# One level of Strassen's algorithm in the w1 and w3 products of a dense feed-forward stack

## The chip, the cores and the metric

One core of one Trainium2 chip runs the whole program. The metric is the device time of one execution in microseconds, as the median over several runs.

## The reference, cut to what matters

The program is a recurrent block with a mixture of experts, and behind it a second block of two layers. Each of these layers has a feed-forward part, a mixer (short convolution, Fourier branch, pooling, gates) and a second feed-forward part. The change concerns the four feed-forward parts.

```python
def swiglu(h, w1, w3, w2):
    return (jax.nn.silu(h @ w1) * (h @ w3)) @ w2

for l in range(DEPTH_2):                       # 2 layers
    h = rmsnorm(x, g_ffn1[l])
    x = x + 0.5 * swiglu(h, w1_a[l], w3_a[l], w2_a[l])
    h = rmsnorm(x, g_mix[l])
    ...
    x = x + merged @ w_o[l]
    h = rmsnorm(x, g_ffn2[l])
    x = x + 0.5 * swiglu(h, w1_b[l], w3_b[l], w2_b[l])
return rmsnorm(x, g_final)
```

There are 512 tokens, the model width is 1024 and the feed-forward width is 2816. Everything is float32.

## The kernel before, in words

**Precision.** A product of float32 is made of three matmuls on reduced-precision operands: each operand is held as a high part and a low part (what the high part leaves), and `mm3` (L170) adds high by high, high by low and low by high. ScalarE casts the high part, VectorE subtracts to get the low part.

**Layout.** Features are on the partitions and the 512 tokens are the columns. The residual x is eight tiles `X[0..7]` of 128 features by 512 tokens. Width 2816 makes 22 feature tiles.

**Weights.** They come as blocks of 128 x 2048 (1 MB) in the order of use; `Stream` (L67) holds the list. `_dma` (L99) issues a block on SP's queue when a raw buffer is free (two of them in the dense phase); `_split` (L119) turns half a block (128 x 1024) into `whi` (ScalarE, L135) and `wlo` (VectorE, L136), in five pairs of buffers; `advance` (L154) is called behind the matmuls on a half and splits as far ahead as the buffers allow, four halves.

**The order of the work** is the order in which the code emits it: each engine runs its own queue in order, and waits where an operand is not ready.

**A feed-forward part** (`ffn`, L1309). The gain is folded into the operand: `prep` (L1213) casts x times gain into `xgh` and `xgl` for each tile as soon as that tile of x is final, and `square` (L1206) sums the squares, ScalarE squaring and POOL adding. `in_chunk` (L1253) multiplies one feature tile of w1 or of w3, eight tiles of x by `mm3`, into one bank. The reciprocal root of the mean square comes late: `rstd_1` (L1226) and `rstd_2` (L1239) run behind the second and third chunk and give `R`, a token a column. For each feature tile VectorE multiplies both products by R (L1334, L1336), ScalarE takes the Silu (L1335), VectorE multiplies (L1337), and `hilo` (L1185) splits the hidden tile. After 12 feature tiles `out_part` (L1261) multiplies them with w2, output tile by output tile, and VectorE adds half of the product to `X[j]` (L1342); then the same with the other 10 tiles. Behind the last addition to a tile the next part's `prep` follows.

**The mixer** (L1347) ends in `out_part2` (L1285), which multiplies four tiles at a time with w_o, the last of the four three output tiles later; VectorE adds to `X[j]` (L1486), and the second feed-forward part's `prep` follows.

**PSUM.** Eight banks, used in turn by `bank` (L1176). SBUF tiles of 128 x 512 come from `tmp` (seven) and `slot` (thirty).

Of the kernel before, what the change touches and what calls it, by code (L numbers as in the profile page):

```python
# [21 lines left out]
S = 512  # L22
# [10 lines left out]
NFA = 12  # L33
L2 = 2
LAG2 = 3
# [31 lines left out]
class Stream:  # L67
    """Weight blocks of 128 x 2048 in the order of use: DMA, then each half as hi + lo."""

    def __init__(self, tc, wpool, nr, nh):  # L70
        self.tc, self.nc = tc, tc.nc
        self.pool = wpool
        self.nh = nh
        self.slots = []
        self.gate = self.hold = 1 << 30
        self.slots_from(wpool, "raw", nr)
        self.blocks = []
        self.raw = {}
        self.half = {}
        self.nb = 0  # L80
        self.ns = 0

    def slots_from(self, pool, tag, n, lo=0, hi=1 << 30, bufs=None):
        """n more raw buffers, for blocks lo to hi"""
        new = [dict(pool=pool, tag=tag, bufs=bufs or n, blk=None, lo=lo, hi=hi) for _ in range(n)]
# [3 lines left out]
    def add(self, aps, keep=()):  # L89
        """keep: blocks that are not split but read as they come"""  # L90
        self.blocks += aps
        self.keep = set(keep)
        self.used = set()

    def _free(self, s):
        b = s["blk"]
        return b is None or (b in self.used if b in self.keep else 2 * b + 1 < self.ns)

    def _dma(self):  # L99
        while self.nb < min(len(self.blocks), self.gate):  # L100
            free = [s for s in self.slots if s["lo"] <= self.nb < s["hi"] and self._free(s)]
# [5 lines left out]
            t = s["pool"].tile([128, BLK], F32, name=s["tag"], tag=s["tag"], bufs=s["bufs"])  # L107
            if self.nb == 0:
                self.first = [lambda a=a, b=b: self.nc.sync.dma_start(t[:, a:b], self.blocks[0][:, a:b])
                              for a, b in FIRST]  # L110
            else:
                self.nc.sync.dma_start(t, self.blocks[self.nb])
# [5 lines left out]

    def _split(self, late=None):  # L119
        h = self.ns  # L120
        if h >= 2 * len(self.blocks):
            return False
        self._dma()
        assert h // 2 < self.nb
        src = self.raw[h // 2][:, (h % 2) * HB:(h % 2 + 1) * HB]
        self.ns += 1
        if h // 2 in self.keep:
# [9 lines left out]
        f() if late is None else late.append(f)  # L137
        return True

    def split_first(self, i):  # L140
        """A piece of the first half"""
# [12 lines left out]
    def advance(self, h, defer=False):  # L154
        """Everything of half h (and before) has been emitted. defer: returns the low parts still to be emitted"""
        late = []
        self.used |= {b for b in self.keep if 2 * b + 1 <= h}
        while self.ns < min(2 * len(self.blocks), self.hold):
            ahead = sum(q // 2 not in self.keep for q in range(h + 1, self.ns + 1))
            if ahead > self.nh - 1 or self.ns // 2 >= self.nb + 1:  # L160
                break
            self._dma()
            if self.ns // 2 >= self.nb:
# [6 lines left out]
def mm3(nc, ps, w, x, first, last):  # L170
    (wh, wl), (xh, xl) = w, x
    nc.tensor.matmul(ps, wh, xh, start=first, stop=False)  # L172
    nc.tensor.matmul(ps, wh, xl, start=False, stop=False)  # L173
    nc.tensor.matmul(ps, wl, xh, start=False, stop=last)  # L174


def build(tc, A):
    nc = tc.nc
    ctx = ExitStack()
    with ctx:  # L180
# [22 lines left out]
        order += [YD[c * 256:(c + 1) * 256].rearrange("(p k) d -> p (k d)", k=2) for c in range(4)]  # L203
        for l in range(L2):
            for n, b in ((N_FFN + 8, None), (N_MIX - 2, A["dfts"])):
                if b is not None:
                    order.append(b)
                order += [wb[i] for i in range(pos, pos + n)]
                pos += n
            order += [wb[i] for i in range(pos, pos + N_FFN)]  # L210
            pos += N_FFN
# [28 lines left out]
        K = dict(tc=tc, A=A, C=C, XP=XP, st=st, vec=vec, vc=vc, vr=vr, ident=ident, onesf=onesf, YD=YD, cs=cs)  # L240
# [47 lines left out]
def rec_phase(K):  # L288
# [256 lines left out]
    # the first of two token tiles is ahead of the second at the end  # L545
# [1175 lines left out]
```

## Time and profile before

| What | us |
|---|---|
| runs, median | 3047.95 |
| runs, lowest and highest | 3045.75, 3051.06 |
| profiled execution, first to last instruction (its span) | 3045.3 |
| TensorE matmuls busy in it | 2972.5 (98%) |
| VectorE busy | 1743.2 (57%) |
| ScalarE busy | 1302.1 (43%) |
| POOL busy | 282.3 (9%) |

The times of the table's last five lines are of one profiled execution, and so are all rows below. Its span is the time from its first to its last instruction; its own device time, as a run would give it, is not listed beside it. Busy shares are means over stages with different limits. A matmul's listed duration includes the time in which its last columns leave the array, so that listed durations of neighbours overlap: how fast matmuls follow each other is read from their starts.

### The profile page before, as it was taken

What the parts mean: (1) busy time and instruction counts of PE and PEld (TensorE: products, weight loads), DVE (VectorE), ACT (ScalarE), POOL (GpSimd) and SP (SyncE); (2) the same over time, 40 slices, a digit from 0 to 9 for tenths busy, and PEclk for the clock granted to TensorE, in tenths of its full rate; (3) what the DMA queues carried; (4) which work ended last, traced back from release to release, by engine and by line L of the source; (5) the groups of instructions that cost most, each with busy time, mean ns of one, the idle gap of its engine ahead of it and who ended that gap; (6) DMA issues with size and microseconds to landing.
All of it is one profiled execution on the core that took longest, in us unless ns stands there. A gap on an engine that the chain in (4) does not pass through costs nothing.

```text
span 3045.3 us, 33566 instructions
## 1 busy us (share of the span) xinstructions
PE 2972.5 (98%) x13360; PEld 2338.3 (77%) x13360; DVE 1743.2 (57%) x2127; ACT 1302.1 (43%) x1687; POOL 282.3 (9%) x235
## 2 busy tenths in 40 slices
PE   9997999999899999999999999999999999999998
PEld 7875666666568888888878888888888888878887
DVE  7678888898974344455555334443344465544343
ACT  4746888888753223233233223322223332332222
POOL 0025222220600000000010000100001000100002
PEclk9998999999999999999999999999999999999999
DMA  6374899999822222222222222222222222232221
GB/s 191 119 277 171 342 363 347 373 371 374 319 80 88 96 97 97 92 81 105 97 97 97 97 97 83 97 97 96 99 83 97 83 97 100 94 109 86 96 97 56
DMA packets 75360, 452.18 MB, mean 148 GB/s; under 512 B 8684, under 2 KB 19308, under 8 KB 22336
## 3 DMA queue, kind: packets, MB, share of 16 engines
q1 hardware_dynamic: 71040, 441.78, 39.4%
q0 software_dynamic: 3072, 7.17, 0.6%
q8 instruction: 106, 1.74, 0.2%
q10 hardware_dynamic: 1088, 1.05, 0.1%
q14 instruction: 54, 0.44, 0.0%
HBM read 439.79 MB, written 14.16 MB: 149 GB/s over the span
## 4 chain that ended last, share of the span: by engine, by line
PE 77%; DVE 4%; ACT 2%; issue 1%; POOL 0%; POOLq 0%; DVEq 0%; ACTq 0%
PE mm L172 23%; PE mm L173 23%; PE mm L174 23%; DVE wlo L136 2%; PE y L857 2%; PE h L822 2%; PE h L821 1%; ACT whi L135 1%; PE ht L835 1%; PE gat L792 1%; DVE xgl L1224 0%; DVE z L1064 0%; DVE X L1486 0%; PE h L824 0%; ACT X L1114 0%
## 5 line engine op out<-in xcount | busy, mean ns | idle before, releaser
L136 DVE TENSOR_TENSOR wlo<-raw,whi 128x1024 fp32r<-128x1024 f32 x533 | 663.9, 1255 | 432.3 <-ACT whi L135 432.3
L172 PE MATMUL mm<-xgh,whi 128*128 128x512 f32 x2048 | 810.6, 396 | 2.2 <-ACT xgh L1218 2.2
L173 PE MATMUL mm<-xgl,whi 128*128 128x512 f32 x2048 | 809.8, 395 | 2.1 <-DVE xgl L1224 2.1
L174 PE MATMUL mm<-xgh,wlo 128*128 128x512 f32 x2048 | 809.2, 395 | 0.0
L135 ACT ACTIVATE whi<-raw 128x1024 fp32r<-128x1024 f32 x535 | 557.9, 1052 | 498.3 <-PE mm L173 457.3
L173 PEld LDWEIGHTS mm<-xgl,whi 128*128 128x128 f32 x2048 | 386.1, 189 | 94.5 <-DVE xgl L1224 4.3
L172 PEld LDWEIGHTS mm<-xgh,whi 128*128 128x128 f32 x2048 | 386.2, 189 | 93.1 <-ACT xgh L1218 2.6
L174 PEld LDWEIGHTS mm<-xgh,wlo 128*128 128x128 f32 x2048 | 386.1, 189 | 90.7
L172 PE MATMUL mm<-s,whi 128*128 128x512 f32 (+1 forms) x938 | 368.0, 392 | 0.0
L173 PE MATMUL mm<-s,whi 128*128 128x512 f32 (+1 forms) x938 | 367.9, 392 | 0.0
L174 PE MATMUL mm<-s,wlo 128*128 128x512 f32 (+1 forms) x938 | 367.8, 392 | 0.0
L1187 ACT ACTIVATE s<-t 128x512 fp32r<-128x512 f32 x128 | 81.0, 633 | 376.2 <-DVE t L1337 298.8
L1211 POOL TENSOR_TENSOR ssum<-ssum,t 128x512 f32<-128x512 f32 x41 | 57.0, 1391 | 1740.2 <-ACT t L1208 1739.5
L136 DVE TENSOR_TENSOR wlo<-rawb,whi 128x1024 fp32r<-128x1024 f32 x162 | 203.6, 1298 | 22.7 <-ACT whi L135 20.6
L172 PEld LDWEIGHTS mm<-s,whi 128*128 128x128 f32 x938 | 176.6, 188 | 40.8
L173 PEld LDWEIGHTS mm<-s,whi 128*128 128x128 f32 x938 | 176.6, 188 | 40.8
L174 PEld LDWEIGHTS mm<-s,wlo 128*128 128x128 f32 x938 | 176.6, 188 | 40.6
L822 PE MATMUL h<-wlo,xt 128*64 128x512 f32 x512 | 195.6, 402 | 7.0 <-DVE wlo L136 6.3
L1336 DVE TENSOR_TENSOR t<-mm,R 128x512 f32<-128x512 f32 x88 | 60.8, 691 | 224.4 <-PE mm L174 224.4
L821 PE MATMUL h<-whi,xt 128*128 128x512 f32 x448 | 181.4, 405 | 5.9 <-PEq L1033 5.0
L1342 DVE SCALAR_TENSOR_TENSOR X<-mm,X 128x512 f32<-128x512 f32 x63 | 43.6, 692 | 227.8 <-PE mm L174 227.8
L857 PE MATMUL y<-whi,hd 128*64 128x512 f32 x512 | 161.6, 397 | 2.5 <-ACT whi L135 1.5
(356 smaller groups left out, 3281.7 us busy)
## 6 DMA issues: line engine op xcount, KB each, us to landing
raw<-in_wblocks SPq DMA_DIRECT2D x265, 1024.0 KB, 4.8
rawb<-in_wblocks SPq DMA_DIRECT2D x81, 1024.0 KB, 6.8
rawa<-in_wblocks SPq DMA_DIRECT2D x57, 1024.0 KB, 6.6
YD<-cs SPq DMA_DIRECT2D x8, 512.0 KB, 7.3
xt<-in_wblocks SPq DMA_DIRECT2D x4, 1024.0 KB, 8.3
rawb<-YD SPq DMA_DIRECT2D x3, 1024.0 KB, 4.8
z<-in_x POOLq DMA_DIRECT2D x4, 512.0 KB, 9.3
raw<-in_dfts SPq DMA_DIRECT2D x2, 1024.0 KB, 4.8
```

What stands on the lines that cost most here:

```text
L135: self.nc.scalar.activation(hi, src, AF.Copy)
L136: f = lambda E=self.nc.vector: E.tensor_tensor(lo, src, hi, op=OP.subtract)
L172: nc.tensor.matmul(ps, wh, xh, start=first, stop=False)
L173: nc.tensor.matmul(ps, wh, xl, start=False, stop=False)
L174: nc.tensor.matmul(ps, wl, xh, start=False, stop=last)
L821: nc.tensor.matmul(ps, x, w[0][:, sl], start=k == 0, stop=False)
L822: nc.tensor.matmul(ps[:64], x[:, 0:64], w[1][:, sl], start=False, stop=False)
L857: nc.tensor.matmul(ps[i][:64], hd[:, f, v:v + 64], w[wv][:, sl], start=f == 0 and n == 0, stop=f == 3 and n == 2)
L1187: act(hi, src, AF.Copy)
L1211: late.append(lambda: E.tensor_tensor(ssum, ssum, t, op=OP.add))
L1336: TT(v, p3, R, op=OP.mult)
L1342: STT(X[j], ps, 0.5, X[j], op0=OP.mult, op1=OP.add)
```

## The change

For a pair of feature tiles of w1 (and of w3) the weights are cut into four quarters of 128 output features by 512 input features, and the input into four quarters of 512 features by 256 tokens. Seven products of sums of quarters replace eight products of quarters (Winograd's form). One such pair is a `group`: seven steps, each with one half block of weights and 4 x 2 x 3 = 24 matmuls of 256 columns, for w1 in the left half of a bank and for w3 in the right.

- **Weights.** `Stream` now has entries that differ from the halves as they lie in memory. For the two blocks p and q of a group it loads q whole and adds half of p to it (an accumulating transfer on POOL's queue); p whole; and half of q with half of p added, into a buffer of half size. Two further sums are made by VectorE in the raw buffer. Seven halves per group are split into high and low, where it was four. There is one more raw buffer of full size and one of half size in a feed-forward part.
- **Inputs.** `forms` makes the sums of quarters of x and their high and low parts, for two tiles of x (k and k + 4) at a time, behind the second one's last addition; `gained` applies the gain, `prep_s` takes the place of `prep` ahead of these parts. The tiles of x are now finished in the order 0, 4, 1, 5, 2, 6, 3, 7.
- **Products.** Three of the seven are accumulated on copies of others, which ScalarE makes from bank to bank; VectorE makes the remaining differences, times R. The end of a group is emitted among the next one's steps.
- **Chunks.** The 22 feature tiles go in chunks of 6, 8 and 8 instead of 12 and 10, and the first two output tiles of a chunk leave their last two hidden tiles for later. The first six tiles of the first feed-forward part keep the old form.
- **Memory.** Six banks in turn and two for the copies; `slot` has 45 tiles, `tmp` five in a feed-forward part and seven in the mixer.

The diff, cut to its core:

```diff
-NFA = 12
+CH = ((0, 6), (6, 14), (14, 22))
+JO = (0, 4, 1, 5, 2, 6, 3, 7)
...
+            p, q = it
+            a = self._block(BLK, (0, BLK, q, False), (0, HB, p[:, HB:], True))
+            b = self._block(BLK, (0, BLK, p, False))
+            c = self._block(HB, (0, HB, q[:, :HB], False), (0, HB, p[:, :HB], True))
+            self._ent(a, 0)
+            self._ent(b, 0)
+            self._ent(a, 0, (b, 0))
+            self._ent(b, 1)
+            self._ent(a, 0, (a, 1))
+            self._ent(c, 0)
+            self._ent(a, 1)
...
-                self.nc.sync.dma_start(t, self.blocks[self.nb])
+                for x, y, src, more in loads:
+                    if more:
+                        self.nc.gpsimd.dma_start(t[:, x:y], src, accum_op=OP.add)
+                    else:
+                        self.nc.sync.dma_start(t[:, x:y], src)
...
         f = lambda E=self.nc.vector: E.tensor_tensor(lo, src, hi, op=OP.subtract)
         f() if late is None else late.append(f)
+        if h + 2 < len(self.ents) and self.ents[h + 2][2]:
+            b2, half2, o = self.ents[h + 2]
+            t, u = self._src(b2, half2), self._src(*o)
+            f = lambda E=self.nc.vector: E.tensor_tensor(t, t, u, op=OP.add)
+            f() if late is None else late.append(f)
...
+def out_order(n):
+    a, b = range(n - 2), range(n - 2, n)
+    return [(JO[0], a), (JO[1], a), (JO[0], b), (JO[1], b)] + [(j, range(n)) for j in JO[2:]]
...
-        return pp.tile([128, 512], F32, name="mm", tag="mm", bufs=8)
+        return pp.tile([128, 512], F32, name="mm", tag="mm", bufs=6)
+    def sbank():
+        return pp.tile([128, 512], F32, name="sv", tag="sv", bufs=2)
...
+    def gained(k, g):
+        if k < 4:
+            XW[k] = wide()
+        act(XW[k % 4][:, k // 4 * S:(k // 4 + 1) * S], X[k], AF.Copy, scale=g(k))
+    def forms(q):
+        x = XW.pop(q).rearrange("p (a b) -> p a b", a=4)
+        p1, p2, p3 = [(slot(), slot()) for _ in range(3)]
...
+        act(halves(p1[0]), x[:, 0::3], AF.Copy, scale=-1.0)
+        s3, s2, s4 = tmp(), tmp(), tmp()
+        xx = x.rearrange("p (k t) b -> p k t b", k=2)
+        TT(halves(s3), xx[:, :, 0], xx[:, :, 1], op=OP.add)
+        TT(s2[:, :256], x[:, 0], x[:, 3], op=OP.add)
+        TT(s2[:, 256:], x[:, 3], x[:, 1], op=OP.subtract)
+        act(p3[0], s3, AF.Copy)
+        act(p2[0], s2, AF.Copy)
+        STT(halves(p1[1]), x[:, 0::3], -1.0, halves(p1[0]), op0=OP.mult, op1=OP.subtract)
+        TT(s4[:, :256], x[:, 2], x[:, 0], op=OP.subtract)
+        act(p4[0], s4[:, :256], AF.Copy)
+        TT(p3[1], s3, p3[0], op=OP.subtract)
+        TT(p2[1], s2, p2[0], op=OP.subtract)
+        TT(p4[1], s4[:, :256], p4[0], op=OP.subtract)
...
+    def prep_s(k, g):
+        gained(k, g)
+        square(k)
+        if k >= 4:
+            late.insert(0, lambda: forms(k - 4))
...
+        def step(i, n, ps, first=False):
+            w = st.get(h + i)
+            for q in range(4):
+                for m in range(2):
+                    sl = slice(m * 512 + q * 128, m * 512 + (q + 1) * 128)
+                    mm3(nc, ps[:, m * 256:(m + 1) * 256], (w[0][:, sl], w[1][:, sl]), XS[n, q],
+                        first and q == 0 and m == 0, q == 3, True)
...
+        pm = bank()
+        step(0, 4, pm, True)
+        pv = sbank()
+        act(pv, pm, AF.Copy)
+        after(0)
+        pz = bank()
+        step(1, 6, pz, True)
+        zs = tmp()
+        act(zs, pz, AF.Copy)
+        if rstd:
+            rstd_1()
+        after(1)
+        step(2, 0, pv)
+        pw = sbank()
+        act(pw, pv, AF.Copy)
+        after(2)
+        if rstd:
+            pr, = rstd_2(0)
+            act(R, pr, AF.Copy)
+        step(3, 2, pm)
+        a = tile()
+        after(3, lambda: STT(a[:, 1], halves(pm), -1.0, RB[1], op0=OP.mult, op1=OP.mult))
+        step(4, 1, pw)
+        vs = tmp()
+        act(vs, pw, AF.Copy)
+        after(4)
+        step(5, 3, pv)
+        after(5, lambda: TT(a[:, 0], halves(pv), halves(zs), op=OP.subtract),
+              lambda: TT(a[:, 0], a[:, 0], RB[0], op=OP.mult))
+        step(6, 5, pw)
+        b = tile()
+        act(a[:, :, 0], a[:, :, 0], AF.Silu)
+        after(6, lambda: TT(b[:, 0], halves(pz), halves(vs), op=OP.subtract),
+              lambda: TT(b[:, 1], halves(pw), RB[1], op=OP.mult))
```

`after(i)` emits what the previous group left over for step i, then the given operations, then `advance`.

## Rows read from the trace of the kernel before

**Rows 1.** The page: the span, and TensorE's busy tenths in 40 slices.
```profile
span 3045.3 us, 33566 instructions
...
PE   9997999999899999999999999999999999999998
```

**Rows 2.** Windows view: w2 and w1/w3 of the last block, and a stretch of full transfers.
```profile
core 0: us, PE busy (x) PEld busy (x) DVE busy (x) ACT busy (x) POOL busy (x), PEclk, DMA share, GB/s
...
2798.00:2866.00 68.00, 68.00 (x293) 54.71 (x292) 21.84 (x23) 14.31 (x14) 0.00 (x0) 1.00 0.26 93
2866.00:2978.00 112.00, 112.00 (x482) 90.09 (x481) 49.42 (x59) 31.90 (x40) 0.00 (x0) 1.00 0.27 94
...
230.00:232.00 2.00, 1.71 (x16) 1.59 (x15) 1.90 (x6) 1.36 (x3) 1.92 (x2) 1.00 0.99 418
```

**Rows 3.** Waits view, TensorE (waited for: us in total, times, longest).
```profile
PE mm L693 <- DVE ohs L688: 14.0, 1, 14.0
...
PE mm L172 <- ACT xgh L1218: 2.2, 1, 2.2
PE mm L173 <- DVE xgl L1224: 2.1, 4, 0.7
```

**Rows 4.** Groups by line and form, TensorE (count, busy us, mean ns, idle before).
```profile
L172 PE MATMUL mm<-s,whi 128*128 128x256 f32 x20 | 5.7, 286 | 0.0
...
L172 PEld LDWEIGHTS mm<-s,whi 128*128 128x128 f32 x938 | 176.6, 188 | 40.8
```

**Rows 5.** Timeline, TensorE: first and last of 26 matmuls (start us, duration us).
```profile
2000.04 0.40 PE L174 MATMUL mm<-xgh,wlo 128*128 128x512 f32 x1
...
2005.86 0.39 PE L172 MATMUL mm<-xgh,whi 128*128 128x512 f32 x1
```

**Rows 6.** Timeline, TensorE, tail: first and last of 45 matmuls of 256 columns.
```profile
3024.57 0.28 PE L172 MATMUL mm<-s,whi 128*128 128x256 f32 x1
...
3029.79 0.28 PE L174 MATMUL mm<-s,wlo 128*128 128x256 f32 x1
```

**Rows 7.** Timeline, VectorE, while w1 and w3 are multiplied.
```profile
2702.29 1.23 DVE L136 TENSOR_TENSOR wlo<-raw,whi 128x1024 fp32r<-128x1024 f32 x1 [2.09 <-ACT whi L135]
2703.43 0.68 DVE L1334 TENSOR_TENSOR t<-mm,R 128x512 f32<-128x512 f32 x1
```

**Rows 8.** Groups by line and form, VectorE.
```profile
L136 DVE TENSOR_TENSOR wlo<-raw,whi 128x1024 fp32r<-128x1024 f32 x533 | 663.9, 1255 | 432.3 <-ACT whi L135 432.3
...
L1460 DVE TENSOR_TENSOR t<-mm,t 128x255 f32<-128x255 f32 x8 | 3.3, 414 | 0.0
```

**Rows 9.** Timeline, VectorE, end of the second layer's mixer; the third beside POOL's sums.
```profile
2656.21 0.68 DVE L1486 TENSOR_TENSOR X<-mm,X 128x512 f32<-128x512 f32 x1
2656.81 0.73 DVE L1224 SCALAR_TENSOR_TENSOR xgl<-X,vec,xgh 128x512 fp32r<-128x512 f32 x1
...
2659.33 1.19 DVE L1224 SCALAR_TENSOR_TENSOR xgl<-X,vec,xgh 128x512 fp32r<-128x512 f32 x1
```

**Rows 10.** Timeline, ScalarE, the same stretch.
```profile
2656.92 0.72 ACT L1218 ACTIVATE xgh<-X,vec 128x512 fp32r<-128x512 f32 x1 [2.37 <-DVE X L1486]
2657.55 0.61 ACT L1208 ACTIVATE t<-X 128x512 f32<-128x512 f32 x1
...
2664.02 1.99 ACT L135 ACTIVATE whi<-raw 128x1024 fp32r<-128x1024 f32 x2
```

**Rows 11.** Transfers by line (count, KB each, median us from issue to landing).
```profile
raw<-in_wblocks SPq DMA_DIRECT2D x265, 1024.0 KB, 4.8
...
z<-in_x POOLq DMA_DIRECT2D x4, 512.0 KB, 9.3
```

**Rows 12.** Timeline, TensorE, first matmuls behind the same mixer, with idle time.
```profile
2664.00 0.50 PE L173 MATMUL mm<-xgl,whi 128*128 128x512 f32 x1 [0.31 <-DVE xgl L1224]
...
2665.70 0.50 PE L173 MATMUL mm<-xgl,whi 128*128 128x512 f32 x1 [0.74 <-DVE xgl L1224]
```

**Rows 13.** Windows view behind TensorE's rest of 14 us (columns as in rows 2).
```profile
248.00:250.00 2.00, 0.22 (x1) 0.25 (x1) 1.68 (x7) 0.00 (x0) 0.79 (x3) 0.50 0.00 0
...
256.00:258.00 2.00, 2.00 (x17) 1.84 (x17) 0.73 (x1) 1.05 (x2) 1.92 (x3) 1.00 0.00 0
```

More of the change, by code (lines that the diff above doesn't have):

```diff
@@ L203, in build, with blocks, count, ffn_blocks @@
         order += [YD[c * 256:(c + 1) * 256].rearrange("(p k) d -> p (k d)", k=2) for c in range(4)]
-        for l in range(L2):
[L205 to L211, printed above, removed]
+        def blocks(n):
+            nonlocal pos
+            pos += n
+            return [wb[i] for i in range(pos - n, pos)]
+        def count(items):
+            return sum(3 if isinstance(i, tuple) else 1 for i in items)
+        sects = []
+        def ffn_blocks(std=False):
+            a = count(order)
+            for f0, f1 in CH:
+                b = blocks(f1 - f0)
+                order.extend(b if std and f0 == 0 else zip(b[0::2], b[1::2]))
+                order.extend(blocks(f1 - f0 >> 1))
+            sects.append((a, count(order)))
+        for l in range(L2):
+            ffn_blocks(l == 0)
+            order += blocks(8)
+            order.append(A["dfts"])
+            order += blocks(N_MIX - 2)
+            ffn_blocks()
         assert pos == nblk, (pos, nblk)
@@ L1264, in out_part @@
         n = 0
-        for j in range(KD):
+        ps = {}
+        for j, ks in out_order(len(x)):
             if tail and j == KD - 1:
@@ L1307, in out_part2, with group, after, tile @@
         h += n // 8
-    def ffn(nxt, pre=None, tail=None):
+    RB = [R[:, None, i * 256:(i + 1) * 256].to_broadcast([128, 2, 256]) for i in range(2)]
+    def group(hid, todo, rstd):
+        nonlocal h
+        def step(i, n, ps, first=False):
[5 more added lines that the diff above has]
+                        first and q == 0 and m == 0, q == 3, True)
+        def after(i, *fs):
+            for f in todo[i:i + 1] + list(fs):
+                f()
+            st.advance(h + i)
+        def tile():
+            return wide().rearrange("p (t m b) -> p t m b", t=2, m=2)
+        pm = bank()
[32 more added lines that the diff above has]
+              lambda: TT(b[:, 1], halves(pw), RB[1], op=OP.mult))
+        h += 7
+        def left(i):
+            if i == 0:
+                TT(b[:, 0], b[:, 0], RB[0], op=OP.mult)
+                act(b[:, :, 0], b[:, :, 0], AF.Silu)
+            if i < 2:
+                t = (a, b)[i]
+                TT(t[:, :, 0], t[:, :, 0], t[:, :, 1], op=OP.mult)
+            if i:
+                hid.append(hilo((a, b)[i - 1][:, :, 0]))
+        return [lambda i=i: left(i) for i in range(3)]
@@ L1348, in mixer @@
         nonlocal h
+        open_mix()
         conv = []
@@ L1377, in mixer @@
             wait = []
-        pu = [bank() for _ in range(4)]
+        pu = [b() for b in (bank, sbank, bank, sbank)]
         for q in range(4):
@@ L1569, in dense_phase @@
     for l in range(L2):
-        ffn(prepper("gmix", l), *[] if l else [squares])
-        mixer(l, prepper("gffn2", l))
-        ffn(*(prepper("gffn1", l + 1),) if l + 1 < L2 else (last, None, tail))
+        ffn(prepper("gmix", l), *[None, None] if l else [squares, None, gain("gffn1", 0)])
+        close()
+        mixer(l, prepper("gffn2", l, prep_s))
+        if l + 1 < L2:
+            ffn(prepper("gffn1", l + 1, prep_s))
+            close()
+            open_ffn(2 * l + 2)
+        else:
+            ffn(last, None, tail)
+    close()
     Dc.__exit__(None, None, None)
```

213 lines of the change are left out of this document (145 added, 68 removed).

## The prediction

> **What bounds the kernel now.** I read the page first: the slices of TensorE stand at 9 or more through the whole dense second half but for the last [rows 1]. The reader is to see one engine that never rests. The windows view then separates the two kinds of stretch of the last feed-forward block: while w1 and w3 are multiplied, TensorE is busy 112.00 of 112 us, VectorE 49.42, ScalarE 31.90, the DMA engines at 0.27 and 94 GB/s; while w2 is multiplied, VectorE has only 21.84 of 68 [rows 2]. The waits view says how little TensorE loses there: its waits for the normalised input (xgh, xgl) are 4.3 us in the whole program [rows 3]. So in these stretches time is the number of matmuls times their spacing.
>
> The listed duration of a matmul is no price: 286 ns for 256 columns, with a weight load of 188 ns each [rows 4]. The starts are. At 512 columns 26 matmuls start between 2000.04 and 2005.86 us, 25 steps in 5.82 us: **232.8 ns** each [rows 5]. At 256 columns the kernel has a run of 45 in its tail, each with its own weight load as in the change: 44 steps from 3024.57 to 3029.79, **118.6 ns** each [rows 6], 0.509 of the wide one. The 188 ns load is hidden under both.
>
> **Term 1, the matmuls.** Two feature tiles of w1 and w3 took 2 x 2 x 8 x 3 = 96 matmuls of 512 columns: 96 x 0.2328 = 22.35 us. A group does the same by 7 x 4 x 2 x 3 = 168 of 256 columns: 168 x 0.1186 = 19.93 us. The first feed-forward block keeps its first six tiles in the old form, so there are 8 + 3 x 11 = 41 groups: 41 x 2.42 = **-99 us**. (Seven eighths alone would give 115; the 1.9% by which two narrow ones exceed a wide one takes the rest.) Nothing covers TensorE here, so all of it is on the path.
>
> Against the change stands a rule of the Trainium skill: "TensorE: Matmul & The Clock Gate", section "Back-to-back issue gap", gives a sustained stream of loads and matmuls about 81 ns at 128 columns and 131 at 512. An estimate between them puts 256 columns near 0.75 of the wide price, which would make a group 168 x 0.75 x 0.2328 = 29.3 us and this term +286 instead of -99. The run of 45 does not agree with it, and the row decides.
>
> **Term 2, splitting and recombining.** Spacing again, not duration: a low part of 128x1024 starts at 2702.29 and the next instruction at 2703.43, so 1.15 us [rows 7], where 1.255 is listed [rows 8]; 512-column operations follow each other after 0.60 [rows 9]. Per group VectorE has 7 low parts where it had 4, two sums of weight quarters (not in the trace; between 0.60, half the columns, and 1.255, the listed low part of the same shape; I take 1.15, the low part's spacing), and ten 512-column operations where it had eight: 9 x 1.15 + 10 x 0.62 = 16.6 us. ScalarE has 7 x 1.0 + 8 x 0.6 = 11.8 [rows 10]. Some 1.5 us a group VectorE must wait for ScalarE, since the Silu of one half stands ahead of a weight split. 18.1 of 19.93: hidden, with 9% left, and I count 0. Were the listed durations the price (9 x 1.255 + 10 x 0.69 + waits of 2.7), a group would last 21 us, so 0 to +45. The copies of products from bank to bank (0.6 us) have one whole step of 24 matmuls (2.85 us) before they are needed: nothing, unless ScalarE is over 2 us late.
>
> **Term 3, the weights' transfers.** A group reads 3.5 MB where it read 2; of these two halves are accumulating transfers from POOL's queue, each behind a plain one into the same buffer. No accumulating transfer is in the trace. 3.5 MB in 20 us is 184 GB/s, under the 418 seen at full use [rows 2]. For one accumulation of 512 KB: below 1.25 us (the bytes at that rate), above 18.6 us (twice the 9.3 us of a plain 512 KB from POOL's queue, as if the old content were a second transfer); I take 9.3, the row it is nearest to [rows 11]. The tightest buffer is the single half-size one: plain part at most 4.8 us (the row of 1 MB), accumulation 9.3, split 2.3, together 16.4 of a period of 19.9. Hidden; it comes into the open at 12.8. On POOL's queue there is behind a waiting accumulation only the next one, and at a block's end sums of squares 5.6 us apart. SP's queue, in the order in which buffers come free, leaves a full-size block over 8 us for its 4.8. The Trainium skill, "Collectives: The Full Stack", section "The bandwidth ceiling: the fold count and why AG ≠ RS ≠ AR", says an adding transfer is slower only because it reads two sources; an estimate from that lets 512 KB move like 1 MB, and the term would stay 0.
>
> **Term 4, from the mixer into the second block, twice.** Here I expect loss. Before, the last residual tile needed one cast and one low part; already there VectorE's instructions stood end to end, and TensorE idled 0.31 and 0.74 us [rows 9, 12]. Now each pair of tiles needs eight VectorE operations (four of 512 columns at 0.62; four of 256, listed 0.41, so about 0.35 [rows 8]): 3.9 us, four times, and the last three tiles are finished only 0.7 us apart. Count VectorE's queue with 0 at the end of w_o. The third tile's update starts at -7.6. From there stand six updates (0.6 each), three sets of forms (3.9) and one weight split with its sum (2.3): 3.6 + 11.7 + 2.3 = 17.6, to 10.0. The low parts wait some 3.6 us for ScalarE, whose gains and squares (0.63 each [rows 10]) stand ahead: 13.6. The last pair then takes gain, square and cast 1.9, handovers 0.2, low part 0.7: 16.4. The group's first step needs exactly this operand for its last quarter (six matmuls): it ends at 17.1 instead of 2.85. That is 14.2; plus about 1, because POOL's sums lengthen VectorE's operations where they overlap (0.73 to 1.19 us [rows 9]); plus 2 for the clock: after a rest of 14 us [rows 3] it was at 0.50 when matmuls came back in 248 to 250, and 1.00 only from 256 [rows 13]; less the 1.05 of before: **+16** each, +32. Bounds: 0 (the forms are hidden after all) and 20 (every overlap with POOL).
>
> **Term 5, other joints.** From one feed-forward block straight into the next (once) tiles come 5.6 us apart and only the last forms are late: update 0.7, gain, square and cast 1.9, low part 0.7, handovers, some 3.8 against 2.1 us of matmuls on the first three quarters, 1.7; and the half-size buffer is opened only then, 16.4 against 16.2 for its use: +3, 0 to 8. The six-tile chunks cover the last hidden tiles with 24 x 0.2328 = 5.6 us and need some 6: 1 each, three times, +3, 0 to 9. The third chunk adds eight 0.6 us updates a block, under w2: nothing. The mixer on six plus two banks: nothing, each bank's reader is done 2 us earlier; were it not, a few us.
>
> **Sum.** -99 + 32 + 3 + 3 = -61, on the profiled execution's span of 3045.3: 2984. The three runs' median of 3047.95 is 2.65 above that span; I carry the 2.65: **2987 us**.
>
> **Rivals.**
> - *The joints hide* (0.10): term 4 falls to 3 each, 2961. For it: VectorE's spare time before the last tiles. Against: it was already full at the end.
> - *VectorE becomes the bound of the groups* (0.15): 21 us a group, +1.1 x 41 = +45, 3032. For it: 9% spare and queues in order. Against: the spacing.
> - *The accumulating transfers decide* (0.10), the one on the slow side. Each is serial with its plain part in one buffer. At 18.6 us the period is 25.7, +5.8 x 41 = +238: 3225. It makes a loss of the change from a period 1.5 us longer, an accumulation above 14.3 us. Against: the nearest row stands 3.5 us under 12.8.
> - *The load of the weights shows at 256 columns* (0.02): 168 x 0.188 = 31.6 us a group, +9.2 instead of -2.4: 3465. Against: the run of 45. The Trainium skill's page on TensorE named above would give 3372.
>
> **How the numbers follow.** The forecast has the remaining 0.63, from 2965 to 3015 with terms 4 and 5 near their bounds. The range reaches through the first rival and to the centre of the second, 2950 to 3035; it leaves out the last two (0.12) and the far part of the second (0.05). A measurement of this kernel can tell about 0.2% (6 us) from none. Faster: 0.63 + 0.10 + 0.10 of the second rival = 0.83; same 0.03 of it; slower its last 0.02 and the 0.12 = 0.14.
>
> **What would show it.** Starts of the 256-column matmuls 0.119 us apart, and 20 us from group to group (term 1); VectorE near 17 of 20 us in the groups' windows (term 2); accumulations landing in under 12.8 us (term 3); behind each mixer a first step that ends some 14 us late, ended by low parts of the forms, under a lowered clock (term 4). I am wrong if groups last 22 us or more with TensorE idle in them, or if those two delays are missing.

## The result, and the profile after

The changed kernel takes **3007.56 us** (median of four runs, 3005.89 to 3008.75), the kernel before, run beside it, 3048.59 (3045.75 to 3051.06). The ratio is 0.9866, with a 95% interval from 0.9852 to 0.9880: 41 us faster, against 61 forecast, inside the range.

From the page of the changed kernel: the span, the engines' busy times (TensorE's matmuls, PE, come first), and TensorE's slices.

```profile
span 3004.9 us, 40511 instructions
...
PE 2891.4 (96%) x16306; PEld 2428.4 (81%) x16306; DVE 2090.3 (70%) x2550; ACT 1535.8 (51%) x2046; POOL 347.5 (12%) x317
...
PE   9997999999889999999999999999999999989998
```

The span is 40.4 us under the 3045.3 of before [rows 1], and TensorE is busy 81.1 us less (2891.4 for 2972.5). So half of what it no longer works came back as 40.7 us of idle time. The windows view of the second chunk of the last block (four groups, then their w2 products) says that it is not in the groups:

```profile
2738.90:2818.60 79.70, 79.70 (x673) 79.70 (x672) 60.75 (x68) 43.20 (x57) 4.32 (x5) 1.00 0.55 161
2818.60:2863.20 44.60, 44.60 (x194) 36.21 (x193) 22.26 (x25) 10.57 (x12) 2.59 (x3) 1.00 0.53 148
```

The columns are length, busy time of PE, PEld, DVE, ACT and POOL, granted clock, DMA share and GB/s. Four groups last 79.70 us, 19.93 each, and TensorE never stops. VectorE is busy 15.2 us of a group, ScalarE 10.8. In place of the rows of transfers [rows 11] now stand, among the DMA issues (size of one, median us to landing), the half-size plain load and the three accumulating ones:

```profile
rawg<-in_wblocks SPq DMA_DIRECT2D x41, 512.0 KB, 3.6
rawg<-in_wblocks POOLq DMA_DIRECT2D x41, 512.0 KB, 6.9
raw<-in_wblocks POOLq DMA_DIRECT2D x22, 512.0 KB, 5.5
rawf<-in_wblocks POOLq DMA_DIRECT2D x19, 512.0 KB, 5.5
```

The idle time is in the waits view of TensorE (us in all, times, longest), where [rows 3] showed 4.3 us for the normalised input:

```profile
PE mm L234 <- ACT s L1346: 27.2, 8, 4.5
PE mm L235 <- DVE s L1354: 11.2, 8, 1.5
...
PE mm L234 <- ACT t L1688: 2.4, 4, 1.0
...
PE mm L234 <- DVE t L1691: 0.6, 2, 0.3
```

L1346 and L1354 are cast and low part of `p1`, the form that the first step of a group reads; L1688 and L1691 read the banks of the mixer's Fourier stage. The first pair is at the three joints. TensorE behind the first mixer (w_o ends at 1560.0), in place of [rows 12]:

```profile
1565.13 0.58 PE L234 MATMUL mm<-s,whi 128*128 128x256 f32 x1 [4.28 <-ACT s L1346]
1567.10 0.58 PE L235 MATMUL mm<-s,whi 128*128 128x256 f32 x1 [1.40 <-DVE s L1354]
1572.50 0.58 PE L234 MATMUL mm<-s,whi 128*128 128x256 f32 x1 [3.96 <-ACT s L1346]
1574.48 0.58 PE L235 MATMUL mm<-s,whi 128*128 128x256 f32 x1 [1.40 <-DVE s L1354]
1578.75 0.58 PE L234 MATMUL mm<-s,whi 128*128 128x256 f32 x1 [2.83 <-ACT s L1346]
1580.86 0.58 PE L235 MATMUL mm<-s,whi 128*128 128x256 f32 x1 [1.53 <-DVE s L1354]
```

Three quarters of the first step come one by one, 6 to 7 us apart. The clock falls meanwhile (columns as above; 0.50 is the lower of its two levels, 1.2 of 2.4 GHz). It was 1.00 from 1560 to 1564, when TensorE's first wait of 4.28 us had begun, and 0.55 in the next 4 us; it is 1.00 again from 1588:

```profile
1576.00:1580.00 4.00, 0.58 (x1) 0.29 (x1) 3.14 (x5) 2.28 (x4) 1.27 (x1) 0.50 0.01 2
...
1584.00:1588.00 4.00, 4.00 (x33) 4.00 (x32) 1.39 (x2) 1.60 (x2) 0.00 (x0) 0.89 0.72 262
```

**How late a joint is.** A chunk of six tiles is three groups of 19.93 and twelve small matmuls for the root mean square, 61.0 us. Behind the first mixer it lasts from 1560.0 to 1641.6, so it is 20.7 late; behind the second 21.6; from block to block 10.9. Before, the mixers' joints lost 1.6 each (the first 48 matmuls of w1 and w3 took 12.76 us behind the second mixer, from 2659.10 to 2671.86, and 11.16 where nothing held them up).

From block to block, VectorE (w2 ends at 1924.7; L1571 updates a tile of x, L1349 begins the forms of a pair), while TensorE waits up to 4.54 us for the last pair's cast (until 1933.65):

```profile
1918.56 0.68 DVE L1571 SCALAR_TENSOR_TENSOR X<-mm,X 128x512 f32<-128x512 f32 x1
1921.49 1.54 DVE L186 TENSOR_TENSOR wlo<-raw,whi 128x1024 fp32r<-128x1024 f32 x1 [2.26 <-ACT whi L185]
...
1924.21 0.68 DVE L1571 SCALAR_TENSOR_TENSOR X<-mm,X 128x512 f32<-128x512 f32 x1
1924.81 0.68 DVE L1349 TENSOR_TENSOR t<-T 128x512 f32<-128x512 f32 x1
...
1932.66 0.69 DVE L1349 TENSOR_TENSOR t<-T 128x512 f32<-128x512 f32 x1 [0.86 <-ACT T L1337]
```

**The account.** In the kernel before, 512-column matmuls of these blocks follow each other after 0.2324 us on average (1560 of them between 1597.29 and 1959.90), a little less than in the forecast's short row, so two tiles took 22.31 us and 41 groups bring 41 x 2.38 = -97.5; joints +19.1, +20.0 and +10.9; the mixers +2.0 and +2.2, from the Fourier stage; and in the third chunk of the three later blocks +0.9 each (their matmuls start 0.1200 us apart on average where the second chunks have 0.1186). Together -40.5, against 40.4 and 41.0 measured.

### The profile page after: what moved, and what is told of

Read it like the earlier page. It is cut to its first block, busy times and chain, and to the rows that moved or that the text cites. A ratio compares the mean times of both kernels' runs of the same rounds, so it can differ in the third digit from the quotient of the medians.

```text
span 3004.9 us, 40511 instructions
## 1 busy us (share of the span) xinstructions
PE 2891.4 (96%) x16306; PEld 2428.4 (81%) x16306; DVE 2090.3 (70%) x2550; ACT 1535.8 (51%) x2046; POOL 347.5 (12%) x317
## 4 chain that ended last, share of the span: by engine, by line
PE 73%; DVE 6%; ACT 3%; issue 1%; DMA 0%; POOL 0%; POOLq 0%; DVEq 0%; ACTq 0%
PE mm L235 15%; PE mm L234 15%; PE mm L236 15%; PE sv L234 7%; PE sv L235 7%; PE sv L236 7%; DVE wlo L186 3%; PE y L936 2%; ACT whi L185 2%; PE h L901 1%; PE h L900 1%; PE ht L914 1%; PE gat L871 0%; DVE s L1354 0%; DVE t L1351 0%
## 5 line engine op out<-in xcount | busy, mean ns | idle before, releaser
L234 PE MATMUL mm<-s,whi 128*128 128x512 f32 (+1 forms) x2464 | 867.3, 352 | 29.9 <-ACT s L1346 27.2
L235 PE MATMUL mm<-s,whi 128*128 128x512 f32 (+1 forms) x2464 | 866.4, 352 | 11.2 <-DVE s L1354 11.2
L236 PE MATMUL mm<-s,wlo 128*128 128x512 f32 (+1 forms) x2464 | 863.8, 351 | 0.0
L234 PEld LDWEIGHTS mm<-s,whi 128*128 128x128 f32 x2464 | 468.5, 190 | 97.3 <-ACT s L1346 29.2
L235 PEld LDWEIGHTS mm<-s,whi 128*128 128x128 f32 x2464 | 468.8, 190 | 78.9 <-DVE s L1354 13.5
L236 PEld LDWEIGHTS mm<-s,wlo 128*128 128x128 f32 x2464 | 469.1, 190 | 65.0
L234 PE MATMUL sv<-s,whi 128*128 128x256 f32 (+1 forms) x1504 | 446.5, 297 | 0.0
L235 PE MATMUL sv<-s,whi 128*128 128x256 f32 (+1 forms) x1504 | 446.3, 297 | 0.0
L236 PE MATMUL sv<-s,wlo 128*128 128x256 f32 (+1 forms) x1504 | 444.7, 296 | 0.0
L236 PEld LDWEIGHTS sv<-s,wlo 128*128 128x128 f32 x1504 | 283.8, 189 | 8.5
L235 PEld LDWEIGHTS sv<-s,whi 128*128 128x128 f32 x1504 | 283.4, 188 | 8.4
L234 PEld LDWEIGHTS sv<-s,whi 128*128 128x128 f32 x1504 | 283.1, 188 | 8.4
L1571 DVE SCALAR_TENSOR_TENSOR X<-mm,X 128x512 f32<-128x512 f32 x95 | 65.3, 688 | 161.3 <-PE mm L236 161.3
L185 ACT ACTIVATE whi<-rawb 128x1024 fp32r<-128x1024 f32 x162 | 163.4, 1055 | 0.1
L186 DVE TENSOR_TENSOR wlo<-rawa,whi 128x1024 fp32r<-128x1024 f32 x114 | 139.0, 1254 | 20.8 <-ACT whi L185 19.2
```

The lines of the kernel that those rows point to most:

```text
L185: self.nc.scalar.activation(hi, src, AF.Copy)
L186: f = lambda E=self.nc.vector: E.tensor_tensor(lo, src, hi, op=OP.subtract)
L234: nc.tensor.matmul(ps, wh, xh, start=first, stop=False, skip_group_check=skip)
L235: nc.tensor.matmul(ps, wh, xl, start=False, stop=False, skip_group_check=skip)
L236: nc.tensor.matmul(ps, wl, xh, start=False, stop=last, skip_group_check=skip)
L1571: STT(X[j], ps, 0.5, X[j], op0=OP.mult, op1=OP.add)
```

## The experiments

All are edits of the changed kernel, compared with runs of the kernel before on the same chip. "Late" is meant as above.

| run | behind mixer 1 | mixer 2 | block to block | median us | ratio to before |
|---|---|---|---|---|---|
| changed kernel | 20.7 | 21.6 | 10.9 | 3007.6 | 0.9866 |
| e1_order | 28.2 | 27.9 | 18.3 | 3031.2 | 0.9948 |
| e2_nosum | 15.1 | 15.7 | 7.0 | 2992.3 | 0.9823 |
| e7_pipe | 18.9 | 19.8 | 8.8 | 3004.6 | 0.9857 |
| e9_pipe_nosum | 13.4 | 12.9 | 8.5 | 2992.0 | 0.9812 |
| e13_nolow | 12.9 | 12.0 | 7.4 | 2988.6 | 0.9800 |

### What makes the joints late

**e1_order** makes only `p1` (`forms_a`) at once and puts the other forms of the last two pairs (`rest`) behind the last update.

```diff
         gained(k, g)
+        if k >= 4:
+            forms_a(k - 4)
         square(k)
-        if k >= 4:
-            late.insert(0, lambda: forms(k - 4))
+        if 4 <= k < KA:
+            late.insert(0, lambda: forms_b(k - 4))
+        if k == KD - 1:
+            qs = range(KA - 4, 4)
+            rest.extend([(f, q) for f in (forms_3, forms_2, forms_4) for q in qs])
```

`KA` is 6, so `qs` is the last two pairs.

> The same work at the three joints in another order: for each pair of tiles only the operand that the group's first step reads (p1: a cast and a low part) is made, straight behind the second tile's gain; the other three forms of the last two pairs are issued behind the last residual update. Theory A (the loss at a joint comes from the order in VectorE's queue, in which the last residual updates stand behind forms that no matmul needs yet): the excess of the first chunk falls from 20.7 and 21.6 us behind the mixers to 4 to 8, from 10.9 between the feed-forward blocks to 4 to 6; in all -30 to -38 us, about 2970 to 2977. Theory B (the loss is the amount of VectorE's work at the joint, which has to be done before the group can go on in any order): the waits only move to the second and third step, within 4 us a joint, 2996 to 3008.

Neither came: every joint is 6 to 8 us later, 0.9948 (0.9931 to 0.9964). VectorE's timeline behind the first mixer in this run (idle time and its releaser at the end of a line):

```profile
1566.45 0.69 DVE L1347 SCALAR_TENSOR_TENSOR s<-T,s 128x512 fp32r<-128x512 f32 x1 [1.45 <-ACT s L1346]
1567.06 0.69 DVE L1756 TENSOR_TENSOR X<-mm,X 128x512 f32<-128x512 f32 x1
1567.66 1.24 DVE L1355 TENSOR_TENSOR t<-T 128x512 f32<-128x512 f32 x1
1569.60 1.38 DVE L1357 TENSOR_TENSOR s<-t,s 128x512 fp32r<-128x512 f32 x1 [0.70 <-ACT s L1356]
```

Each low part stands straight behind its own cast, so VectorE waits 0.5 to 1.5 us for ScalarE at each of them, with the next residual updates queued behind it. The emission order of the change, sums first and low parts last, had hidden these handovers. And two operations (L1355 and the L1357 behind it) take 1.24 and 1.38 us, where such operations take 0.69 elsewhere.

**e2_nosum** asks what that second effect is worth.

```diff
-        if k:
+        if k and add:
             late.append(lambda: E.tensor_tensor(ssum, ssum, t, op=OP.add))
...
-        square(k)
+        square(k, add=False)
```

> Leaves out the seven additions of squares on POOL at each of the three joints into a block in the new form (the sum then holds the first tile's squares alone); order and forms as in the changed kernel. Theory C (POOL's additions lengthen VectorE's operations, and this is the part of the loss that the forecast of 16 had too small): the forms' VectorE operations that now take 1.4 to 1.75 us fall to 0.4 to 0.7 us, and the excess behind a mixer falls from 20.7 to 13 to 15 us; between the feed-forward blocks from 10.9 to 9 or more, since additions there stand 5.6 us apart; in all -12 to -16 us, about 2992 to 2996. Rival (POOL doesn't matter, the queue's length does): under 2 us a joint, 3002 to 3008.

Theory C holds behind the mixers, with 5.6 and 5.9 us less; from block to block the additions cost 3.9, twice what was expected. The ratio is 0.9823 (0.9806 to 0.9839), 15.3 us less in all. Behind the first mixer, where w_o ends at 1558.7 in this run, the last wait of the first step ends with this matmul:

```profile
1574.37 0.58 PE L235 MATMUL mm<-s,whi 128*128 128x256 f32 x1 [0.38 <-DVE s L1354]
```

Four more follow, so that the step ends at 1575.6, 14.1 us late. Three of VectorE's operations on one pair, in the changed kernel:

```profile
1563.55 0.42 DVE L1350 TENSOR_TENSOR t<-T 128x256 f32<-128x256 f32 x1
1563.88 1.49 DVE L1351 TENSOR_TENSOR t<-T 128x256 f32<-128x256 f32 x1
1565.30 1.75 DVE L1354 SCALAR_TENSOR_TENSOR s<-T,s 128x512 fp32r<-128x512 f32 x1
```

and without POOL's additions:

```profile
1560.70 0.42 DVE L1350 TENSOR_TENSOR t<-T 128x256 f32<-128x256 f32 x1
1561.04 0.42 DVE L1351 TENSOR_TENSOR t<-T 128x256 f32<-128x256 f32 x1
1562.27 0.69 DVE L1354 SCALAR_TENSOR_TENSOR s<-T,s 128x512 fp32r<-128x512 f32 x1 [0.81 <-ACT s L1346]
```

0.42 and 0.69 us became 1.49 and 1.75, about 1.07 more for each addition. Part of that hid a wait of 0.81 for ScalarE, so 7 additions cost 5.6 us and not 7.5.

The Trainium skill, "SBUF — State Buffer", section "Who interferes with whom", says that a VectorE instruction with two SBUF inputs contends with a GpSimd instruction that reads SBUF, and calls the ports that the two engines share "an exclusive lock". The trace agrees: each of the operations above, with both inputs in SBUF, is longer by nearly one of POOL's additions (1.27 us where one stands alone, at 1578.32).

The full price was in the trace before, just ahead of the rows that the forecast read [rows 9]. VectorE and POOL in the kernel before:

```profile
2652.24 1.81 DVE L1224 SCALAR_TENSOR_TENSOR xgl<-X,vec,xgh 128x512 fp32r<-128x512 f32 x1
```

```profile
2652.20 1.31 POOL L1211 TENSOR_TENSOR ssum<-ssum,t 128x512 f32<-128x512 f32 x1 [144.34 <-ACT t L1208]
```

The low part that took 0.73 us alone took 1.81 beside a whole addition.

**e7_pipe** reorders in stages: behind the update of each of the eight tiles, and behind the last, it emits what this list says (c1 is a cast of `p1`, l1 its low part, s3 a sum with its cast, l3 its low part, sq a square with POOL's addition; the figure is the pair, or the tile). Behind a mixer:

```diff
+        True: ((), ((c1, 0),), ((l1, 0), (s3, 0), (s2, 0), (s4, 0)), ((c1, 1), (l3, 0), (l2, 0), (l4, 0)),
+               ((l1, 1), (s3, 1), (s2, 1), (s4, 1)), ((c1, 2),), (), ((c1, 3), (l1, 2), (l3, 1)),
+               ((s3, 2), (l1, 3), (s3, 3), (sq, 6), (l2, 1), (s2, 2), (l3, 2), (sq, 3), (l3, 3), (s2, 3),
+                (sq, 7), (l4, 1), (l2, 2), (s4, 2), (l2, 3), (s4, 3), (l4, 2), (l4, 3))),
```

> The first order fell: with each low part issued straight behind its own cast, VectorE waited 0.7 to 1.5 us for ScalarE at every operand. Now the same work in stages: an operand's low part is issued at least one other VectorE operation behind the one that feeds its cast; p1 of every pair first, and behind a mixer the other forms of the last three pairs and the last three squares behind all residual updates. Theory A (order and handovers decide, the amount would fit): first step late by 4 to 5 us, later steps by 2 more, so excess 5 to 8 behind the mixers (20.7 and 21.6 in the changed kernel), 4 to 6 between the blocks (10.9): 3007.6 - 33 = about 2972 to 2980. Theory B (the amount of VectorE's work between the last tiles and the third step decides, with POOL's additions lengthening it): excess 12 or more behind the mixers, 2988 to 3005.

Theory B: 2 us a joint, 0.9857 (0.9841 to 0.9874), which cannot be told from the change itself. Behind a mixer the first step does end 8 us earlier (14.0 us behind w_o instead of 22.1), but TensorE then waits for what was put later, the sum of squares last:

```profile
1572.82 0.58 PE L234 MATMUL mm<-s,whi 128*128 128x256 f32 x1 [3.69 <-ACT s L1347]
1584.47 1.05 PE L1438 MATMUL mm<-onesf,ssum 128*128 128x2 f32 x8 [3.64 <-POOL ssum L1319]
```

**e9_pipe_nosum** is e7 with POOL's additions left out.

> The staged order of the last experiment on it, with POOL's seven additions of squares left out at each joint (the sum then holds the first tile's squares alone). The staged order alone gave 18.9 and 19.8 us behind the mixers, of which 5 were TensorE waiting for the sum of squares that it had put last; the additions alone gave 15.1 and 15.7. Theory A (order and POOL together are the loss): 6 to 10 us behind the mixers, 4 to 6 between the blocks, in all about 2972 to 2982. Theory B (VectorE's own amount of work is the loss, POOL only comes on top): 13 to 15 behind the mixers, 6 to 7 between the blocks, the same as without the additions in the changed kernel's order: 2990 to 2994.

Theory B behind the mixers: late by 13, where the staged order is worth 2 to 3 us. Between the blocks neither theory holds: 8.5, which is 1.5 more than without it. With another 1.6 lost in the first block, the time is that of e2.

**e13_nolow** is e2 with three of VectorE's eight operations a pair left out.

```diff
-        p1, p2, p3 = [(slot(), slot()) for _ in range(3)]
+        p1 = (slot(), slot())
+        p2, p3 = [(slot(), p1[1]) for _ in range(2)]
...
-        TT(p3[1], s3, p3[0], op=OP.subtract)
-        TT(p2[1], s2, p2[0], op=OP.subtract)
-        TT(p4[1], s4[:, :256], p4[0], op=OP.subtract)
```

> The changed kernel's order, POOL's seven additions of squares left out at each joint as before, and in addition the low parts of the forms p2, p3 and p4 left out (their products take p1's low part instead). Of each pair's eight VectorE operations five stay; 0.60 + 0.60 + 0.34 = 1.55 us less a pair. Theory B (behind a mixer VectorE is busy from before the last tiles to the last low part, so its work there is the loss, microsecond for microsecond): three pairs stand ahead of the last p1, 4.6 us less, 15.1 and 15.7 fall to about 10.5 and 11. Rival (ScalarE's casts or the handovers set the end, and VectorE's lows hide beside them): 14 or more, as with the additions alone left out.

Between the two: 4.6 us of VectorE's work removed give back 2.2 and 3.7 behind the mixers, nothing (+0.4) between the blocks. So VectorE's work there is part of the loss, but not microsecond for microsecond. The windows view of this run (columns as above: DVE is the third busy time, ACT the fourth) shows which engine is full now:

```profile
1564.00:1568.00 4.00, 1.81 (x6) 1.32 (x6) 3.57 (x7) 3.76 (x8) 0.00 (x0) 0.60 0.00 0
1568.00:1572.00 4.00, 2.01 (x6) 1.43 (x6) 2.40 (x6) 3.76 (x8) 0.00 (x0) 0.50 0.00 0
```

In the changed kernel VectorE was busy 4.00 and 3.81 us of these four, ScalarE 2.54 and 2.44; here it is ScalarE, 3.76 of 4, with two gains, two squares and four casts a pair. A pair costs VectorE 5.1 us (two updates and the forms, 1558.62 to 1564.75 in e2_nosum, less 1.0 of waits) and ScalarE 4.4 (1561.32 to 1565.72 in e13_nolow), beside the weights' splits; behind a mixer the pairs are complete 5.6, 3.5 and 1.4 us apart. No order that was tried keeps up with that.

### VectorE's margin inside the groups

**e8_margin** adds VectorE work whose output nobody reads.

```diff
             for f in todo[i:i + 1] + list(fs):
                 f()
+            if i < 6:
+                TT(R2, R, R, op=OP.mult)
```

> Adds six VectorE products of 128x512 (0.61 us by their spacing) to each of the 41 groups, one behind each of the first six steps; their output is read by nobody in the feed-forward blocks. VectorE goes from 15.2 to 18.9 us of the 19.93 of a group. If a group's limit is VectorE's sum of work alone, the groups stay at 19.93 and the time at 3008 to 3016 (the first groups behind the joints are late by up to 2 us more each). If the waits of VectorE for ScalarE that the forecast put at 1.5 us a group stand in the way: 18.9 + 1.5 = 20.4, +0.5 x 41 = +20, about 3028; with forecast figures throughout (18.1 + 3.7 = 21.8): +77, 3085.

Nothing happens, not even the few us at the joints: 3006.9 us, 0.9866 (0.9849 to 0.9882). The four groups of the last block's second chunk:

```profile
2735.90:2815.70 79.80, 79.80 (x674) 79.76 (x673) 72.33 (x90) 41.76 (x55) 4.32 (x5) 1.00 0.53 157
```

VectorE is busy 91% (18.1 us a group), and TensorE still never waits. The rival in which VectorE bounds the groups was further off than the forecast thought. In this run the third chunks have 0.1186 us a matmul too, so those 2.8 us are not VectorE's either.

### The mixers' banks

**e4_banks** gives the first pair of the Fourier stage's outputs the two reserved banks.

```diff
-            p1, p2 = bank(), bank()
+            p1, p2 = [b() for b in ((bank, bank) if g else (sbank, sbank))]
```

> The two banks reserved for products take the first pair of outputs of the mixer's Fourier stage, so that its eight outputs stand in eight banks as in the kernel before. If the stage waits only because six banks turn instead of eight: its waits for ScalarE's and VectorE's readers (2.4 and 0.6 us in all) disappear, and the mixers get back 2.2 us each, 3007.6 - 4.4 = about 3003. Rival (the stage is late for another reason, such as ScalarE's own queue): the waits stay, 3006 to 3008.

No gain, 0.9877 (0.9860 to 0.9893): the wait moved from inside the stage to its end. TensorE in the changed kernel:

```profile
1329.09 0.50 PE L234 MATMUL mm<-s,csh 128*128 128x512 f32 x1 [0.96 <-ACT t L1688]
1330.37 0.35 PE L234 MATMUL mm<-s,csh 128*128 128x256 f32 x1 [0.32 <-DVE t L1691]
1331.21 0.50 PE L234 MATMUL mm<-s,whi 128*128 128x512 f32 x1 [0.25 <-ACT t L1688]
```

and in e4:

```profile
1332.19 0.51 PE L234 MATMUL mm<-s,whi 128*128 128x512 f32 x1 [2.04 <-ACT t L1688]
```

This is the gate's product behind the stage: the ring of six has come round to the second pair, which ScalarE hasn't read yet. In the kernel before, the ninth allocation met the first pair. **e6_old2_banks** gives the reserved banks to the second pair (`g == 1`), so that it meets the first again. The same run tries the next question.

### Forms away from the joints

**e3_std**: six tiles of every block in the old form, as in the first block.

```diff
-            ffn_blocks(l == 0)
+            ffn_blocks(True)
...
-        mixer(l, prepper("gffn2", l, prep_s))
+        mixer(l, prepper("gffn2", l))
...
-            ffn(prepper("gffn1", l + 1, prep_s))
+            ffn(prepper("gffn1", l + 1), None, None, gain("gffn2", l))
```

> The first six tiles of all four feed-forward blocks in the old form (as the changed kernel has them in the first block only), so that the forms are made under the w2 products that follow. If the loss sits in the joints alone and the forms hide under w2: the joints lose 19.3 + 20.3 + 10.9 = 50.5 us, nine groups at 2.42 more cost 21.8, so 3007.6 - 50.5 + 21.8 = about 2979, with 1.4 us left behind each mixer. Rival (the forms don't fit under w2 either, and the wait moves there): an excess of 5 us or more in the w2 part behind each first chunk, 2994 or more.

2984.4, 0.9794 (0.9777 to 0.9810): the forms hide under w2, and behind the mixers 2 to 4 us are lost instead of 21. The joints' loss is that of making the forms there.

**e6_old2_banks**: only two tiles in the old form, the forms made under them, and the banks as said.

```diff
+                for f in range(m):
+                    for b in (bank, sbank):
+                        wait.append(in_r(b))
+                        q = len(wait) - 1
+                        if m == 2:
+                            for k in (q, q + 4):
+                                gained(k, std)
+                            forms(q)
...
-            p1, p2 = bank(), bank()
+            p1, p2 = [b() for b in ((sbank, sbank) if g == 1 else (bank, bank))]
```

> Only the first two tiles (not six) of the second, third and fourth feed-forward block in the old form, the forms made under their four chunks of 5.6 us; the two reserved banks go to the second instead of the first pair of outputs of the mixer's Fourier stage, so that nine allocations pass before a bank comes round, as in the kernel before. If the forms hide under 22.35 us of old products: joints lose 50.5, three groups at 2.42 more cost 7.3, some 1.4 stays at each joint: about 3007.6 - 50.5 + 7.3 + 3 = 2967, and 4.4 less, 2963, if the mixers' waits go with the bank order. Rival (VectorE can't make four sets of forms in 22 us beside the low parts of the weights and the sums of squares): the first group behind the two tiles starts 5 us or more late, three times, 2978 or more. For the banks: the stage's waits (3.0 us in all) under 0.5, or unchanged if ScalarE is simply late.

2988.9, 0.9803 (0.9787 to 0.9820). The bank order works: the stage's wait is gone from the waits view, and each mixer is 2.1 us shorter. For the forms the rival came: the group behind the two tiles is late by 9.6, 9.0 and 8.0. That two tiles are too few is not shown by it: in TensorE's waits view 10.6 us of these (three waits, 4.4 the longest) are for the copy from bank to bank, the wait that the next runs take up, and two tiles were not tried again without it.

**e11_std_banks** is e3 with that bank order.

> The first six tiles of every block in the old form, forms made under the w2 products behind them, and the bank order that took the mixers' waits away: 2984.4 less 4.4, about 2980, if the two gains add; 2984 if the bank order only helped because something else was late.

2976.7, 0.9761 (0.9748 to 0.9775): the gains add, to within 3 us. The order of the banks is the only difference to e3, and the Fourier stage falls from 95.9 us to 93.7.

**e10_old4_banks**: four tiles in the old form, forms under their eight chunks.

> The first four tiles of the second, third and fourth block in the old form, forms made under their eight chunks (44.7 us, where 22.35 were too short by 8 to 10), and the bank order that took the mixers' waits away. If the forms fit now: against six tiles of the old form (2984.4) three groups more in the new form give 7.3, the mixers 4.4: about 2973. Rival (the last pair's forms, whose buffers are those of the normalised input and come free with the eighth chunk only, hold up the first group by 3 us or more, three times): 2981 or more.

2985.2, 0.9794 (0.9780 to 0.9807): the rival, late by 7 us three times. TensorE, and ScalarE ahead of it:

```profile
1616.12 0.58 PE L234 MATMUL sv<-s,whi 128*128 128x256 f32 x1 [4.03 <-ACT sv L1513]
```

```profile
1612.90 0.63 ACT L1295 ACTIVATE s<-T 128x512 fp32r<-128x512 f32 x1 [0.57 <-DVE T L1584]
1614.95 0.63 ACT L1295 ACTIVATE s<-T 128x512 fp32r<-128x512 f32 x1 [1.42 <-DVE T L1584]
1615.49 0.58 ACT L1513 ACTIVATE sv<-mm 128x512 f32<-128x512 f32 x1
```

The copy from bank to bank (L1513) stands behind casts of the old tiles (L1295) that wait for VectorE. So it was a queue again, and one that can be reordered.

**e12_old4_split** puts those casts, and `p4` of the last pair, behind steps 0 and 1 of the group, and the rest of that pair's forms behind the Silus. The cut is against e10:

```diff
-            for u, v in uv:
-                TT(u, u, v, op=OP.mult)
-                hid.append(hilo(u))
+            return [lambda i=i: out(i) for i in range(len(uv))]
...
-                lambda: run((s3, 3), (s2, 3), (l3, 3), (l2, 3), (s4, 3), (l4, 3)))
+                lambda: s3(3))
```

> Four tiles in the old form again, with two things taken out of ScalarE's way: in the last run of this kind the copy of the first product to its second bank stood in ScalarE's queue behind the silu products' casts of tiles two and three, and TensorE waited 4.2 us for it, three times. Now these casts, and p4 of the last pair, come behind the first and second step of the group, the other forms of the last pair ahead of them. If that order was the wait: excess of the first group from 7 to 2 to 3 us, three times, 2985.2 - 13 = about 2972, below the 2976.7 of six tiles. Rival (VectorE's and ScalarE's work behind the eighth chunk is too much for the first two steps in any order): 5 us or more stay, 2979 or more.

**2971.7 us**, 0.9746 (0.9733 to 0.9760). The wait is now

```profile
1618.79 0.39 PE L234 MATMUL sv<-s,whi 128*128 128x256 f32 x1 [0.67 <-ACT sv L1524]
```

and the group is late by under 1 us. This version beats both kernels, by 78 us and 36; over e11 its lead is 5 us, with intervals that still overlap.

## Why the prediction was right, and where it wasn't

- **Term 1, the matmuls: right.** 19.93 us a group, as forecast to the hundredth; the old price was 22.31 and not 22.35, so the term is -97.5. The estimate of 29.3 from the Trainium skill's issue gap ("TensorE: Matmul & The Clock Gate", section "Back-to-back issue gap") does not hold here: 118.6 ns on average over 672 matmuls in a row.
- **Term 2: right at nothing**, and safer than it said: 15.2 us of VectorE in place of 16.6, and six operations more cost nothing (e8). The listed durations, its upper end, were the wrong price.
- **Term 3: right.** Accumulations landed after 5.5 and 6.9 us (medians) where 9.3 was taken and 12.8 allowed. The slow-side rival fell with that.
- **Term 4: the mechanism right, one summand mis-sized.** Forecast +16 a joint with an upper bound of 20, measured +19.1 and +20.0. The queue was right item by item: without POOL's additions (e2) VectorE goes through the six updates, the three sets of forms, the split and its sum in the order forecast, with 2.6 us of waits for ScalarE (forecast 3.6), and the first step ends 14.1 us late behind both mixers (forecast 14.2). The clock's part is about 2 and 3 us: 20 and 30 matmuls behind the last wait are 0.214 us apart. What was mis-sized is "plus about 1, because POOL's sums lengthen VectorE's operations": they cost 5.6 and 5.9 (e2). The row it came from, 0.73 to 1.19 us [rows 9], showed an operation that an addition overlapped in part; here each of the seven additions stops one operation for nearly its full length.
- **Term 5: the joint from block to block was wrong**, +3 (0 to 8) against +10.9. The step "tiles come 5.6 us apart and only the last forms are late" failed. VectorE was behind already: w2 finished the seventh tile at 1919.1 (24 matmuls ahead of its end at 1924.7), and VectorE updated it at 1924.21, so that the forms of the third pair started only as the first group did, and those of the fourth at 1932.66. Two pairs were open and not one. It falls behind because two tiles take VectorE 12.6 us there (1911.62 to 1924.21) and w2 only 11.2. In these 12.6 it idles 2.9, of them 2.26 for the high part of a weight, which ScalarE casts behind the gain and the square of the tile just updated; the next update stands behind that weight's low part. Of the 10.9 POOL's part is 3.9 (e2), the clock's 2.0 (20 matmuls); that the handovers make up the other 5 is likely by this row, but no run took them away alone. The six-tile chunks, put at +1 each, cost nothing.
- **"The mixer on six plus two banks: nothing"** was wrong by 4.2 us, which is the "few us" of its own proviso. The readers are done in time for a ring of eight, not of six; e11 takes the loss away by the order of the banks alone.
- **Not forecast:** the third chunks' 0.1200 us a matmul, 2.8 in all. In e8 none of these chunks has it, in e7 and e12 one of three, with the same matmuls in them; its cause is open.

The sum missed by 20 us: 7 at the mixers' joints, 8 at the other, 4.2 in the mixers, 2.8 in the third chunks, 1.5 in term 1, less the 3 of the six-tile chunks.

## What to carry to other kernels

When a cheaper algorithm needs its operands in a new form, cost the places where a stage begins, not only the steady state: there the new work of all tiles falls due at once. Give such a place something to do that needs no new form (here four tiles the old way in three blocks, 3 x 2 x 2.38 = 14.3 us dearer; with the banks it saved 36 in all), and then look which copy or cast stands in the queue behind work that isn't urgent. Moving buffers between pools changes which reader an allocation waits for, even if their number stays the same.

## What the runs showed of the hardware

- POOL's 128x512 addition (1.27 us alone) stops a VectorE operation with two SBUF inputs for about 1.07 us, whether that takes 0.42 or 0.69 by itself (1.49 and 1.75, e2 beside the changed kernel).
- An accumulating transfer of 512 KB into SBUF, from POOL's queue, lands after 5.5 to 6.9 us in the median, a plain one of that size from SP's queue after 3.6. What of this is the queue's was not tried.
- In some chunks the 672 matmuls start 120.0 ns apart on average instead of 118.6, at the same granted clock (1.00); unexplained.
